# Tokens as the stationary operand in 26 projection calls, an overflow branch ahead of the final norm, and a longer ring for the expert weights

## The chip, the cores and the metric

The kernel runs on one core of a Trainium2 chip. The metric is the device time of one execution, in microseconds (us). Before the change it is 1512.69 us, the median of 3 runs (1511.3 to 1512.91). The engines are called PE (TensorE matmul; PEld is its weight load), DVE (VectorE), ACT (ScalarE), POOL (GpSimd) and SP (SyncE, which here issues almost all DMAs).

## The reference, cut to what matters

The program computes two decoder layers over 256 tokens of width 1024, all in float32, and a last RMSNorm. Layer 0 ends in a dense SwiGLU, layer 1 in a top-2-of-8 expert SwiGLU.

```python
for layer in range(DEPTH):                       # DEPTH = 2
    h = rms_norm(x, norm_mix[layer])
    # nine projections of h: q, f, i, g (1024 wide), b, c, u (1024), gate_a, gate_b (1024)
    ...
    o = rms_norm(hgrn2(q, k, i, log_f), g_norm_w) * silu(g)
    y_a = o @ w_proj_hgrn
    y_b = (c * causal_conv3(b * u)) @ w_proj_conv
    merged = sigmoid(gate_a) * y_a + sigmoid(gate_b) * y_b
    x = x + merged @ w_out
    h = rms_norm(x, norm_ffn[layer])
    if layer % 2 == 0:
        x = x + (silu(h @ dense_w1) * (h @ dense_w3)) @ dense_w2        # D_FF = 2816
    else:                                        # each token goes to 2 of 8 experts
        x = x + sum_e gates[:, e] * ((silu(h @ w1[e]) * (h @ w3[e])) @ w2[e])
return rms_norm(x, final_norm)
```

The weights are 414 MB in float32, 277 MB of them the experts'.

## The kernel before

**Dense products.** A weight matrix is read in pieces of 1 MB. `wload` (line 77) takes a buffer from a ring (`from_ring`), issues the DMA on SP's queue, and splits the piece into a high part on ACT (line 91, tile `whi`) and a low part on DVE (line 93, tile `wlo`). The activations are split the same way (`hh`, `hl`), so each product is three matmuls: high by high, high by low, low by high. There are two forms.

- `mm_cols` (line 125): 128 x 128 of the weights are stationary and the 256 tokens move through them. The result has the output columns on the partitions (tile `psb`). One call on 512 columns is 8 k-tiles x 4 column blocks x 3 parts = 96 matmuls, each 256 wide.
- `mm_toks` (line 151): 128 x 128 of the activations are stationary and 512 weight columns move. The result has the tokens on the partitions (tile `psa`): 8 k-tiles x 2 token halves x 3 parts = 48 matmuls, each 512 wide.

Before, `mm_toks` serves the HGRN value and output-gate projections and `w_out`. `mm_cols` serves the rest: forget gates, queries, the convolution's b, c, u, the two merge gates (lines 577 to 583), the two projections (lines 620 to 637) and the dense w1 and w3 (lines 713 to 723). The down projection of the dense layer (`down`, line 700) has its own loops of 512-wide matmuls.

In the column form the factor `rstd` of a token lies along the free axis, so DVE multiplies by a broadcast row (`by_rbc`, line 256) ahead of the sigmoid or silu. In the token form it is one number per partition and rides in the ACT instruction as its scale.

**Buffers.** Matmul results come from a PSUM tag `mm` with two buffers. The split weights come from `his` (three buffers, tag `hi`) and `los` (two, tag `lo`). A scheduler lays the instructions of each engine out in a fixed order; each engine, and SP's queue, takes them in that order.

**The expert layer.** `moe` (line 775) sorts the experts into eight slots `q` with room for 96 or 64 tokens each (96, 64, 96, 96, 64, 96, 96, 64). Tokens are gathered by one-hot matmuls (`gather`, for slot 0, and at slots 0, 3 and 6 for the next up to three slots), the weights stream as moving operands straight from their raw pieces (`up_proj` line 975, `down` line 987), and the results are scattered back by one-hot matmuls (`scatter` line 1007). A slot reads 34.6 MB whatever its room. The pieces lie in a ring of raw buffers; a piece's DMA is issued on SP as soon as PE has finished with the buffer's last piece. From line 781 on the ring has 11 buffers: the four of `raws`, and the tags qq, fc, v, tokA, sg8, kk and tokB of the large tiles that are free by then. The tag kk holds `xw` of the router (line 458) until then.

**The end.** After the last scatter `finish` (line 754) makes the last norm and writes the output in four DMAs on SP. Then every engine loads two counts (line 1067): they say whether any expert had more tokens than its slot has room for. If so, `slots(1)` and `slots(2)` are run, each followed by another `finish`. With these inputs neither is. The instructions of the two bodies lie between the branch and its target on every engine.

Of the kernel before, what the change touches and what calls it, by code (L numbers as in the profile page):

```python
# [13 lines left out]
ALU = mybir.AluOpType  # L14
# [22 lines left out]
def trunk_kernel(ctx: ExitStack, tc: tile.TileContext, x, w_in, lower_bounds, hgrn_norm_w, conv_w,  # L37
# [32 lines left out]
    def from_ring(kind, pool, shape, dt):  # L70
        tag = ring[kind][0]
        ring[kind].rotate(-1)
        if tag is None:
            return pool.tile(shape, dt, tag=kind, name="w" + kind)
        return big.tile(shape, dt, tag=tag, name="w" + kind)
# [143 lines left out]
    def transposed(src, j):  # L219
        ps = psum.tile([128, 2, S], F32, tag="so"[j % 2], name="pst")  # L220
# [229 lines left out]
    def route_start(l):  # L450
# [5 lines left out]
        moe_ps["wb"] = big8("bu", [128, D])  # L456
        nc.gpsimd.dma_start(moe_ps["wb"], bc_row(norm_ffn[l], D))
        moe_ps["xw"] = big8("kk", [128, TT, D])
# [20 lines left out]
    def route_rows(t, half):  # L479

        xw, hh, hl = (moe_ps[n] for n in ("xw", "hh", "hl"))
        cs = slice(half * 512, half * 512 + 512)
        nc.vector.tensor_tensor(xw[:, t, cs], xt[:, t, cs], moe_ps["wb"][:, cs], op=ALU.mult)
        nc.scalar.activation(hh[:, t, cs], xw[:, t, cs], AF.Copy)

    def route_low(t, half):
        xw, hh, hl = (moe_ps[n] for n in ("xw", "hh", "hl"))
        cs = slice(half * 512, half * 512 + 512)
        nc.vector.tensor_tensor(hl[:, t, cs], xw[:, t, cs], hh[:, t, cs].bitcast(F32), op=ALU.subtract)
# [25 lines left out]
    def mixer(l):  # L515
# [104 lines left out]
        for g in range(2):  # L620
            ps = mm_cols(w_proj_conv[l], g * 512, 512, ych, ycl)
            gs = slice(g * 4, g * 4 + 4)
            nc.vector.tensor_tensor(sg[8][:, gs, :], sg[8][:, gs, :], ps, op=ALU.mult)
# [6 lines left out]
        mh, ml = (big8(tag, [128, KT, S], F32R) for tag in ("hlC", "hlD"))  # L630
        for g in range(2):
            ps = mm_cols(w_proj_hgrn[l], g * 512, 512, oh, ol)
            for i in range(2):
                gs = slice(g * 4 + i * 2, g * 4 + i * 2 + 2)
                nc.vector.tensor_tensor(sg[7][:, gs, :], sg[7][:, gs, :], ps[:, i * 2:i * 2 + 2, :], op=ALU.mult)
                nc.vector.tensor_tensor(sg[7][:, gs, :], sg[7][:, gs, :], sg[8][:, gs, :], op=ALU.add)
                split(sg[7][:, gs, :], mh[:, gs, :], ml[:, gs, :])
# [3 lines left out]
        for g in range(2):  # L641
# [10 lines left out]
            if g == 0:  # L652
                ps = mm_toks(w_out[l], 0, mh, ml)
# [35 lines left out]
    def dense(l):  # L689
# [22 lines left out]
        lo_, hi_ = slice(0, 512), slice(512, 1024)  # L712
        for ci, (c0, n) in enumerate(FCH):
            nt = n // 128
            pa = mm_cols(dense_w1[j], c0, n, hh, hl, enter if ci == 0 else {})
            sa = big8(("fc", "kk")[ci % 2], [128, nt, S])
            by_rbc(sa, pa)
            nc.scalar.activation(sa, sa, AF.Silu)
            pb = mm_cols(dense_w3[j], c0, n, hh, hl)
            nc.vector.tensor_tensor(sa, sa, pb, op=ALU.mult)  # L720
            ah = big8(("qq", "v")[ci % 2], [128, nt, S], F32R)
            al = big8(("bu", "sg7")[ci % 2], [128, nt, S], F32R)
            split(sa, ah, al)
# [5 lines left out]
            else:  # L729

                def add(dh):
                    cs = (lo_, hi_)[dh]
                    for t in range(TT):
                        nc.vector.scalar_tensor_tensor(xt[:, t, cs], ys[t * 2 + dh], rstd[:, t:t + 1], xt[:, t, cs],
                                                       op0=ALU.mult, op1=ALU.add)
# [15 lines left out]
            pend = (c0, n, ah, al)  # L751


    def finish():
# [4 lines left out]
        for t in range(TT):  # L759
            for dh in range(2):  # L760
# [3 lines left out]
                nc.sync.dma_start(osrc[:, t, cs], fin[:, t, cs])  # L764
# [10 lines left out]
    def moe(l):  # L775
# [5 lines left out]
        less("kk")  # L781
        more("kk", "tokB")
# [4 lines left out]
        cnt = consts.tile([128, 1], F32, name="cnt")  # L787
# [28 lines left out]
        def late():  # L816
# [31 lines left out]
            for i in range(2):  # L848
# [4 lines left out]
                nc.vector.tensor_reduce(cnt, over, axis=AX.X, op=ALU.max)  # L853
                nc.vector.tensor_copy(orderi[:, i:i + 1], cnt)
# [32 lines left out]
        ids = {0: 0}  # L887

# [6 lines left out]
        def slots(base):  # L895
# [91 lines left out]
            def down(q, c0, n, th, ys):  # L987
# [12 lines left out]
                if c0 + n == FF:  # L1000
                    y = los.tile([128, 2, 3 * 256], F32R, tag="lo", name="y")
# [5 lines left out]
            def scatter(q, y):  # L1007
                PT = one_hot_t(q)
                for dh in range(2):
                    cs = slice(dh * 512, dh * 512 + 512)  # L1010
                    for t in range(TT):
# [15 lines left out]
                        if q == NE - 1:  # L1027
                            square(t, dh, "kk")
# [8 lines left out]
            for q in range(NE):  # L1037
                xf = xfs[q]
                ys = [psum.tile([128, 512], F32, tag="o", name="ye") for _ in range(2 if CAPS[q] == 96 else 1)]
                for ci, (c0, n) in enumerate(ECH):  # L1040
# [6 lines left out]
                    up_proj(expert_w3, c0, n, pb, xf, q)  # L1047
                    if ci == 1:
# [4 lines left out]
                    sa = his.tile([128, ng, n // 4], F32, tag="hi", name="sae")  # L1053
                    nc.scalar.activation(sa, pa[:, 0:ng, 0:n // 4], AF.Silu)  # L1054
                    nc.vector.tensor_tensor(sa, sa, pb[:, 0:ng, 0:n // 4], op=ALU.mult)  # L1055
                    th = his.tile([128, nb, ng, 32], F32, tag="hi", name="the")
# [52 lines left out]
```

## Time and profile before

| what | us |
|---|---|
| median of 3 runs | 1512.69 |
| the profiled execution's own time | 1511.85 |
| its span, first to last instruction | 1510.1 |
| PE busy in the span | 1462.3 |
| DVE / ACT / POOL busy | 651.4 / 394.4 / 41.7 |
| start of the first expert matmul | 809.4 |
| start of the last expert piece's first matmul | 1489.2 |

The profiled execution takes 1.75 us more than its span; the median of the runs lies 0.84 us above it. The table of slices on the page shows two parts. Up to about 810 us PE is busy throughout and the DMA engines about half. From there on the DMA engines are busy nearly throughout, at some 410 GB/s, and PE as well by its busy time; but a matmul's record reaches to its modelled end, so a busy PE may still be waiting for weights between two matmuls.

### The profile page before, as it was taken

Reading aid. Unit: us, or ns where it says so; the run is one execution under the profiler, and the core shown is the slowest. Engines: PE = TensorE matmul, PEld = TensorE weight load, DVE = VectorE, ACT = ScalarE, POOL = GpSimd, SP = SyncE. Lnnn points to the kernel's source line nnn. Section 1 sums busy time; section 2 is a strip of 40 time slices with the busy share of each in tenths; the row PEclk is TensorE's granted clock in tenths of the full one; section 3 lists DMA queues with packets and bytes.
Section 4 is the critical chain, followed back from the end, with each engine's and each line's share of the span. In section 5 each row is a group of like instructions: output and inputs, shape, how many; then the busy total and the mean of one; then the engine's idle time right before and its main releaser. Section 6 shows DMA issues by size and latency. Waiting matters only on the chain.

```text
span 1510.1 us, 39658 instructions
## 1 busy us (share of the span) xinstructions
PE 1462.3 (97%) x18130; PEld 1203.4 (80%) x18130; DVE 651.4 (43%) x875; ACT 394.4 (26%) x484; POOL 41.7 (3%) x80
## 2 busy tenths in 40 slices
PE   7999999999999999999999999899999989999994
PEld 7989999999999998999996696557977554766751
DVE  6965776665455796568764202011121102011112
ACT  6544334454344554434442000000000000000000
POOL 3000011000000000001000000000000000000000
PEclk9999999999999999999999999999999999999998
DMA  8564544556556555555746899999999999999994
GB/s 270 181 194 157 169 140 170 194 168 195 186 178 197 166 194 170 168 168 203 285 168 226 290 402 409 410 413 406 411 373 402 408 413 409 408 412 359 411 410 184
DMA packets 135364, 418.15 MB, mean 277 GB/s; under 512 B 6784, under 2 KB 8928, under 8 KB 123920
## 3 DMA queue, kind: packets, MB, share of 16 engines
q1 hardware_dynamic: 134768, 414.26, 73.9%
q8 instruction: 146, 2.39, 0.7%
q0 software_dynamic: 384, 1.21, 0.3%
q14 instruction: 34, 0.28, 0.1%
q10 hardware_dynamic: 32, 0.01, 0.0%
HBM read 414.40 MB, written 1.05 MB: 275 GB/s over the span
## 4 chain that ended last, share of the span: by engine, by line
PE 89%; DMA 9%; DVE 1%; ACT 0%; issue 0%; SPq 0%; POOL 0%; POOLq 0%; DVEq 0%; ACTq 0%
PE psb L139 12%; PE pa L982 12%; PE psb L143 12%; PE psb L141 12%; PE pb L982 11%; PE ye L972 10%; DMA wraw<-in_expert_w_dram 8%; PE psa L160 3%; PE psa L162 3%; PE psa L161 3%; PE psc L1023 2%; PE y L708 1%; PE y L709 1%; PE y L710 1%; PE pg L920 1%; PE ye L964 1%
## 5 line engine op out<-in xcount | busy, mean ns | idle before, releaser
L139 PE MATMUL psb<-hlA,whi 128*128 128x256 f32 x1376 | 393.5, 286 | 3.2 <-ACT whi L91 3.2
L143 PE MATMUL psb<-hlA,wlo 128*128 128x256 f32 x1376 | 390.4, 284 | 0.8 <-DVE wlo L93 0.8
L141 PE MATMUL psb<-hlB,whi 128*128 128x256 f32 x1376 | 390.2, 284 | 0.0
L91 ACT ACTIVATE whi<-wraw 128x2048 fp32r<-128x2048 f32 (+1 forms) x165 | 251.7, 1543 | 376.6 <-PE psb L141 234.5
L93 DVE TENSOR_TENSOR wlo<-wraw,whi 128x2048 fp32r<-128x2048 f32 (+1 forms) x165 | 297.9, 1821 | 116.3 <-issue 40.4
L139 PEld LDWEIGHTS psb<-hlA,whi 128*128 128x128 f32 x1376 | 264.3, 192 | 4.6 <-ACT whi L91 3.6
L143 PEld LDWEIGHTS psb<-hlA,wlo 128*128 128x128 f32 x1376 | 264.2, 192 | 1.5 <-DVE wlo L93 1.3
L141 PEld LDWEIGHTS psb<-hlB,whi 128*128 128x128 f32 x1376 | 264.5, 192 | 0.5
L1055 DVE TENSOR_TENSOR sae<-sae,pb 128x768 f32<-128x768 f32 (+3 forms) x24 | 19.1, 796 | 454.5 <-PE pb L982 454.5
L972 PE MATMUL ye<-wraw,the 128*32 128x256 f32 x2640 | 150.5, 379 | 1.0 <-issue 1.0
L972 PEld LDWEIGHTS ye<-wraw,the 128*32 128x32 f32 x2640 | 104.8, 110 | 39.9 <-issue 2.5
L1054 ACT ACTIVATE sae<-pa 128x768 f32<-128x768 f32 (+3 forms) x24 | 16.4, 685 | 433.1 <-PE pa L982 433.1
L982 PE MATMUL pb<-wraw,bu 128*32 128x256 f32 (+1 forms) x2112 | 109.3, 362 | 2.4 <-DMA wraw<-in_expert_w_dram 1.8
L982 PE MATMUL pa<-wraw,bu 128*32 128x256 f32 (+1 forms) x2112 | 110.0, 362 | 0.7 <-DMA wraw<-in_expert_w_dram 0.7
L982 PE MATMUL pb<-wraw,hlD 128*32 128x256 f32 (+1 forms) x1920 | 100.8, 362 | 4.0 <-DMA wraw<-in_expert_w_dram 3.9
L982 PE MATMUL pa<-wraw,hlD 128*32 128x256 f32 (+1 forms) x1920 | 102.2, 362 | 0.7 <-DMA wraw<-in_expert_w_dram 0.7
L982 PEld LDWEIGHTS pb<-wraw,bu 128*32 128x32 f32 x2112 | 74.7, 110 | 34.3 <-issue 2.8
L982 PEld LDWEIGHTS pa<-wraw,bu 128*32 128x32 f32 x2112 | 73.2, 110 | 34.0 <-issue 4.9
L982 PEld LDWEIGHTS pb<-wraw,hlD 128*32 128x32 f32 x1920 | 71.3, 110 | 30.3 <-DMA wraw<-in_expert_w_dram 5.8
L982 PEld LDWEIGHTS pa<-wraw,hlD 128*32 128x32 f32 x1920 | 72.8, 110 | 26.3 <-issue 6.4
L964 PE MATMUL ye<-wraw,the 128*64 128x512 f32 x264 | 61.8, 601 | 10.7 <-DMA wraw<-in_expert_w_dram 10.7
L964 PEld LDWEIGHTS ye<-wraw,the 128*64 128x64 f32 x264 | 17.2, 136 | 51.2 <-issue 27.1
(259 smaller groups left out, 1459.3 us busy)
## 6 DMA issues: line engine op xcount, KB each, us to landing
wraw<-in_expert_w_dram SPq DMA_DIRECT2D x216, 1024.0 KB, 17.8
wraw<-in_w_in_dram SPq DMA_DIRECT2D x72, 1024.0 KB, 5.2
wraw<-in_expert_w_dram SPq DMA_DIRECT2D x64, 768.0 KB, 15.9
wraw<-in_dense_w_dram SPq DMA_DIRECT2D x33, 1024.0 KB, 5.1
wraw<-in_w_proj_conv_dram SPq DMA_DIRECT2D x8, 1024.0 KB, 5.1
wraw<-in_w_proj_hgrn_dram SPq DMA_DIRECT2D x8, 1024.0 KB, 5.1
wraw<-in_w_out_dram SPq DMA_DIRECT2D x8, 1024.0 KB, 5.2
xt<-in_x_dram SPq DMA_DIRECT2D x2, 512.0 KB, 3.8
```

Source lines behind the costliest of these rows:

```text
L91: nc.scalar.activation(hf[:, ks], rf[:, ks], AF.Copy)
L93: nc.vector.tensor_tensor(lf[:, ks], rf[:, ks], hf[:, ks].bitcast(F32), op=ALU.subtract)
L139: nc.tensor.matmul(o, wh[:, k, cs], hh[:, kt, :], start=first, stop=False, skip_group_check=True)
L141: nc.tensor.matmul(o, wh[:, k, cs], hl[:, kt, :], start=False, stop=False, skip_group_check=True)
L143: nc.tensor.matmul(o, wl[:, k, cs], hh[:, kt, :], start=False, stop=last, skip_group_check=True)
L160: nc.tensor.matmul(o, hh[:, kt, ts], wh[:, k, :], start=kt == 0, stop=False)
L161: nc.tensor.matmul(o, hh[:, kt, ts], wl[:, k, :], start=False, stop=False)
L162: nc.tensor.matmul(o, hl[:, kt, ts], wh[:, k, :], start=False, stop=kt == KT - 1)
L964: nc.tensor.matmul(out[64 * h:64 * h + 64, 0:n], stat, w[:, h * n:h * n + n], start=start, stop=stop, skip_group_check=True)
L972: nc.tensor.matmul(out(g)[32 * lane:32 * lane + 32, 0:n], by_lane(g if lane == 3 else lane, lane), w[:, c0:c0 + n], start=start and g != 1 ...
L982: nc.tensor.matmul(ps[32 * lane:32 * lane + 32, g, 0:n // 4], xf[:, kt, 32 * g:32 * g + 32], w[:, k, lane * n // 4:(lane + 1) * n // 4], s ...
L1023: nc.tensor.matmul(ps[:, o], PT[:, w, ts], y[:, part, c], start=i == part == 0, stop=part == 1 and i in (0, 3), skip_group_check=True)
```

## The change

- The two merge gates, the two projections and the five 512-wide chunks of dense w1 and w3 use `mm_toks` in place of `mm_cols`: 4 + 4 calls in each layer and 10 in the dense layer, 26 in all. Sigmoid and silu take `rstd` as ACT's scale, read PSUM and write SBUF.
- What then has tokens on its partitions but is wanted as a stationary operand with columns on them is transposed by PE: the merged branch (`merged`, 4 groups of 4 transposes in each layer, at k-tiles 3 and 5 of the second `w_proj_hgrn` call and at k-tiles 1 and 2 of the first `w_out` call), and each dense chunk (`turn`, 8 transposes at k-tile 3 of the next chunk's w1 call). The transposed tiles are split out of PSUM.
- The dense layer's `rstd` goes into w3's eviction in place of the last addition.
- The router's `xw` shrinks to half a row and shares a tile with `wb`, so kk stays in the ring. In `moe` sg8 leaves the ring (it takes the scattered results `y`), and the three `hi` buffers come in: 13 buffers where there were 11. The tiles `sa` and `th` move from `his` to two tiles of `los`.
- Overflow is told in one number (0, 1 or 2). One branch on it stands ahead of `finish`, with the second nested in it, and there is one `finish`. Its DMAs go half to SP, half to ACT. The last slot scatters one token half after the other.

```diff
-        less("kk")
-        more("kk", "tokB")
+        less("sg8")
+        more("hi", "hi", "hi", "tokB")
+        work = [los.tile([128, 2, 768], F32, tag="lo", name="work") for _ in range(2)]
...
-            sg[s] = big8(f"sg{s}", [128, KT, S])
+            sg[s] = big8(f"sg{s}", [128, TT, D])
             for g in range(2):
-                ps = mm_cols(wi, col(s, g), 512, hh, hl)
-                gs = slice(g * 4, g * 4 + 4)
-                by_rbc(sg[s][:, gs, :], ps)
-                nc.scalar.activation(sg[s][:, gs, :], sg[s][:, gs, :], AF.Sigmoid)
+                ps = mm_toks(wi, col(s, g), hh, hl)
+                for t in range(TT):
+                    nc.scalar.activation(sg[s][:, t, g * 512:g * 512 + 512], ps[:, t, :], AF.Sigmoid, scale=rstd[:, t:t + 1])
...
+        def merged(j):
+            ps = transposed(sg[7], j, "s")
+            split(ps, mh[:, 2 * j:2 * j + 2, :], ml[:, 2 * j:2 * j + 2, :])
+
         for g in range(2):
-            ps = mm_cols(w_proj_hgrn[l], g * 512, 512, oh, ol)
...
+            ps = mm_toks(w_proj_hgrn[l], g * 512, oh, ol,
+                         {3: [lambda: merged(0)], 5: [lambda: merged(1)]} if g == 1 else {})
+            for t in range(TT):
+                cs = slice(g * 512, g * 512 + 512)
+                nc.vector.tensor_tensor(sg[7][:, t, cs], sg[7][:, t, cs], ps[:, t, :], op=ALU.mult)
+                nc.vector.tensor_tensor(sg[7][:, t, cs], sg[7][:, t, cs], sg[8][:, t, cs], op=ALU.add)
+        late_cols = {1: [lambda: merged(2)], 2: [lambda: merged(3)]}
...
-                ps = mm_toks(w_out[l], 0, mh, ml)
+                ps = mm_toks(w_out[l], 0, mh, ml, late_cols)
...
+        def turn(pend):
+
+            c0, n, sa, ah, al = pend
+            ps = psum.tile([128, 4, S], F32, tag="mm", name="pst")
+            for k in range(4):
+                for t in range(TT):
+                    nc.tensor.transpose(ps[:, k, t * 128:t * 128 + 128], sa[:, t, k * 128:k * 128 + 128], ident)
+            for i in range(2):
+                split(ps[:, 2 * i:2 * i + 2, :], ah[:, 2 * i:2 * i + 2, :], al[:, 2 * i:2 * i + 2, :])
...
+            if n == 512:
+                pa = mm_toks(dense_w1[j], c0, hh, hl, steps)
+                for t in range(TT):
+                    nc.scalar.activation(sa[:, t, :], pa[:, t, :], AF.Silu, scale=rstd[:, t:t + 1])
+                pb = mm_toks(dense_w3[j], c0, hh, hl)
+                for t in range(TT):
+                    nc.vector.scalar_tensor_tensor(sa[:, t, :], pb[:, t, :], rstd[:, t:t + 1], sa[:, t, :],
+                                                   op0=ALU.mult, op1=ALU.mult)
...
-                nc.sync.dma_start(osrc[:, t, cs], fin[:, t, cs])
+                (nc.sync, nc.scalar)[dh].dma_start(osrc[:, t, cs], fin[:, t, cs])
...
+                    if q == 4 and ci == 1 and base == 0:
+                        left.append(nc.values_load(orderi[0:1, 0:1], min_val=0, max_val=2))
...
         slots(0)
+        with tc.If(left[0] > 0):
+            slots(1)
+            with tc.If(left[0] > 1):
+                slots(2)
         finish()
-        left = [nc.values_load(orderi[0:1, i:i + 1], min_val=0, max_val=S) for i in range(2)]
-        for base in (1, 2):
-            with tc.If(left[base - 1] > 0):
-                slots(base)
-                finish()
```

How the order of instructions moves is shown at three places. The first is PE in the dense layer, chunk 1's w1 call (hlA, hlB are the split activations). Before, around its middle:

```order
L139 MATMUL psb<-hlA,whi 128x256
L141 MATMUL psb<-hlB,whi 128x256
L143 MATMUL psb<-hlA,wlo 128x256
L139 MATMUL psb<-hlA,whi 128x256
L141 MATMUL psb<-hlB,whi 128x256
```

And now, where `turn` of chunk 0 (its product in fc) stands in it:

```order
L163 MATMUL psa<-wlo,hlA 128x512
L164 MATMUL psa<-whi,hlB 128x512
L727 MATMUL pst<-ident,fc 128x128 x8
L162 MATMUL psa<-whi,hlA 128x512
L163 MATMUL psa<-wlo,hlA 128x512
```

Each matmul is twice as wide, there are half as many, and eight transposes stand between the two weight pieces of the call.

The second is DVE in layer 0 around `w_proj_hgrn` (sg_1156 is sg[7], the merged branch; hlD its low part). Before:

```order
L623 TENSOR_TENSOR sg_1426<-sg_1426,psb 128x1024
L93 TENSOR_TENSOR wlo<-wraw,whi 128x2048 x2
L635 TENSOR_TENSOR sg_1156<-sg_1156,psb 128x512 x2
L636 TENSOR_TENSOR sg_1156<-sg_1156,sg_1426 128x512 x2
L93 TENSOR_TENSOR wlo<-wraw,whi 128x2048
L56 TENSOR_TENSOR hlD<-sg_1156,hlC 128x512 x2
```

Now:

```order
L625 TENSOR_TENSOR sg_1330<-sg_1330,psa 128x2x512
L95 TENSOR_TENSOR wlo<-wraw,whi 128x2048 x2
L643 TENSOR_TENSOR sg_1156<-sg_1156,psa 128x512 x2
L644 TENSOR_TENSOR sg_1156<-sg_1156,sg_1330 128x512 x2
L95 TENSOR_TENSOR wlo<-wraw,whi 128x2048
L56 TENSOR_TENSOR hlD<-pst,hlC 128x512 x2
L95 TENSOR_TENSOR wlo<-wraw,whi 128x2048
L643 TENSOR_TENSOR sg_1156<-sg_1156,psa 128x512 x2
L644 TENSOR_TENSOR sg_1156<-sg_1156,sg_1330 128x512 x2
L56 TENSOR_TENSOR hlD<-pst,hlC 128x512 x2
```

The operations and their sizes are the same, but the low part is now taken from PE's transposed tile `pst`, and before the second pair (L643, L644) a weight split stands.

The third is DVE at the end of the program. Before, from the last scatter's split to the first branch:

```order
L56 TENSOR_TENSOR y<-ye,y 128x512
L1025 SCALAR_TENSOR_TENSOR xt<-psc,qgates,xt 128x512 x4
L196 SCALAR_TENSOR_TENSOR rstd<-msq 128x1
L762 SCALAR_TENSOR_TENSOR bu<-xt,rstd,wbf 128x512
L196 SCALAR_TENSOR_TENSOR rstd<-msq 128x1
L762 SCALAR_TENSOR_TENSOR bu<-xt,rstd,wbf 128x512 x3
L1067 TENSOR_LOAD orderi
L1069 COMPARE_AND_BRANCH
```

Now, from the same split on; the branch jumps over both bodies to what the next block shows:

```order
L1099 STREAM_TRANSPOSE work<-work 128x6x32 x2
L56 TENSOR_TENSOR sg_13795<-ye,sg_13795 128x512
L1062 SCALAR_TENSOR_TENSOR xt<-psc,qgates,xt 128x512 x4
L1086 TENSOR_LOAD orderi
L1107 COMPARE_AND_BRANCH
```

```order
L1109 UNCONDITIONAL_BRANCH x2
L1107 UNCONDITIONAL_BRANCH
L198 SCALAR_TENSOR_TENSOR rstd<-msq 128x1 x2
L791 SCALAR_TENSOR_TENSOR bu<-xt,rstd,wbf 128x512 x4
L1144 UNCONDITIONAL_BRANCH
```

The load of the count and the branch stand between the last addition and the norm, on every engine, though the source asks for the load in slot 4.

## Rows read from the trace of the kernel before

**Rows 1.** The page: busy times, and DMA rate in 40 slices of 37.75 us.

```profile
PE 1462.3 (97%) x18130; PEld 1203.4 (80%) x18130; DVE 651.4 (43%) x875; ACT 394.4 (26%) x484; POOL 41.7 (3%) x80
GB/s 270 181 194 157 169 140 170 194 168 195 186 178 197 166 194 170 168 168 203 285 168 226 290 402 409 410 413 406 411 373 402 408 413 409 408 412 359 411 410 184
```

**Rows 2.** Longest wait of PE from 10 to 809 us: total, times, longest.

```profile
PE psb L139 <- ACT whi L91: 3.2, 1, 3.2
```

**Rows 3.** Timeline of PE (start, us, instruction): 42 wide steps, then 53 narrow ones.

```profile
359.78 0.39 PE L710 MATMUL y<-whi,bu 128*128 128x512 f32 x1
...
369.30 0.39 PE L710 MATMUL y<-whi,bu 128*128 128x512 f32 x1
369.53 0.28 PE L139 MATMUL psb<-hlA,whi 128*128 128x256 f32 x1
...
375.88 0.28 PE L143 MATMUL psb<-hlA,wlo 128*128 128x256 f32 x1
```

**Rows 4.** Timeline of PE: eight transposes within a token call.

```profile
304.93 1.04 PE L224 MATMUL pst<-ident,xt 128*128 128x128 f32 x8
305.72 0.48 PE L160 MATMUL psa<-whi,hlC 128*128 128x512 f32 x1
306.04 0.40 PE L161 MATMUL psa<-wlo,hlC 128*128 128x512 f32 x1
```

**Rows 5.** Timeline of DVE after a `w_proj_hgrn` call (start, us, instruction).

```profile
288.77 1.28 DVE L635 TENSOR_TENSOR sg<-sg,psb 128x512 f32<-128x512 f32 x2 [3.42 <-PE psb L143]
289.98 1.29 DVE L636 TENSOR_TENSOR sg<-sg,sg 128x512 f32<-128x512 f32 x2
291.18 2.29 DVE L93 TENSOR_TENSOR wlo<-wraw,whi 128x2048 fp32r<-128x2048 f32 x1
```

**Rows 6.** A group by line and form: busy us, mean ns, idle before.

```profile
L562 ACT ACTIVATE v<-psa,rstd 128x512 f32<-128x512 f32 x8 | 5.1, 686 | 13.7 <-PE psa L162 13.7
```

**Rows 7.** Stretches of 30 us in the expert layer: busy, PEclk, DMA share, GB/s.

```profile
850.00:880.00 30.00, 30.00 (x555) 24.46 (x551) 6.57 (x10) 1.58 (x4) 0.00 (x0) 1.00 0.76 276
1030.00:1060.00 30.00, 29.89 (x649) 26.39 (x645) 2.13 (x4) 0.65 (x1) 0.00 (x0) 1.00 1.02 409
1110.00:1140.00 30.00, 29.96 (x560) 24.52 (x562) 6.42 (x10) 1.58 (x4) 0.00 (x0) 1.00 0.92 353
1370.00:1400.00 30.00, 30.00 (x578) 22.45 (x580) 4.37 (x10) 1.37 (x4) 0.00 (x0) 1.00 0.92 349
```

**Rows 8.** Timeline of SP's queue: expert pieces 11 and 12 to 14 are issued.

```profile
806.01 0.37 SPq L99 DMA_DIRECT2D wraw<-in_expert_w_dram  x1
812.26 5.55 SPq L99 DMA_DIRECT2D wraw<-in_expert_w_dram  x3
```

**Rows 9.** Timeline of the end, from the last scatter's matmuls on.

```profile
1491.88 2.14 PE L1023 MATMUL psc<-y,st 128*128 128x512 f32 x8 [0.76 <-ACT y L55]
1493.36 2.73 DVE L1025 SCALAR_TENSOR_TENSOR xt<-psc,qgates,xt 128x512 f32<-128x512 f32 x4 [0.81 <-PE psc L1023]
...
1496.41 0.16 DVE L196 SCALAR_TENSOR_TENSOR rstd<-msq 128x1 f32<-128x1 f32 x1 [0.32 <-ACT junk L191]
...
1497.30 0.75 DVE L762 SCALAR_TENSOR_TENSOR bu<-xt,rstd,wbf 128x512 f32<-128x512 f32 x1 [0.73 <-POOL rstd L197]
1499.23 1.41 DVE L762 SCALAR_TENSOR_TENSOR bu<-xt,rstd,wbf 128x512 f32<-128x512 f32 x2 [0.45 <-POOL rstd L197]
```

**Rows 10.** The instructions of lines 1069, 1104, 764: ns min/median/max, first and last start.

```profile
L1069 DVEq COMPARE_BRANCH  x2: 56/64/72, 1499.9 to 1503.5; - x2
L1069 DVEq EVENT_SEMAPHORE  x2: 21/21/21, 1503.0 to 1506.6; - x2
L1069 SPq EVENT_SEMAPHORE  x16: 17/17/17, 1504.8 to 1508.5; - x16
L1104 SPq EVENT_SEMAPHORE  x13: 17/28/28, 1508.6 to 1510.1; - x13
DMA to landing us min/median/max: 2.9/3.9/4.2
```

More of the change, by code (lines that the diff above doesn't have):

```diff
@@ L74, in from_ring @@
             return pool.tile(shape, dt, tag=kind, name="w" + kind)
+        if tag == "hi":
+            return his.tile(shape, dt, tag=tag, name="w" + kind)
         return big.tile(shape, dt, tag=tag, name="w" + kind)
@@ L217, in to_cols, with transposed @@
         return hh, hl
-    def transposed(src, j):
-        ps = psum.tile([128, 2, S], F32, tag="so"[j % 2], name="pst")
+    def transposed(src, j, tag=None):
+        ps = psum.tile([128, 2, S], F32, tag=tag or "so"[j % 2], name="pst")
         for i in range(2):
@@ L712, in dense @@
         lo_, hi_ = slice(0, 512), slice(512, 1024)
+        def turn(pend):
[6 more added lines that the diff above has]
+                split(ps[:, 2 * i:2 * i + 2, :], ah[:, 2 * i:2 * i + 2, :], al[:, 2 * i:2 * i + 2, :])
         for ci, (c0, n) in enumerate(FCH):
             nt = n // 128
[L715 to L720, printed above, removed]
+            steps = dict(enter) if ci == 0 else {3: [lambda p=pend: turn(p)]}
+            pend = pend and (*pend[:2], *pend[3:])
+            sa = big8(("fc", "kk")[ci % 2], [128, TT, n])
             ah = big8(("qq", "v")[ci % 2], [128, nt, S], F32R)
             al = big8(("bu", "sg7")[ci % 2], [128, nt, S], F32R)
-            split(sa, ah, al)
+            if n == 512:
[6 more added lines that the diff above has]
+                                                   op0=ALU.mult, op1=ALU.mult)
+            else:
+                sa = sa.rearrange("p t c -> p (t c)").rearrange("p (k s) -> p k s", s=S)
+                pa = mm_cols(dense_w1[j], c0, n, hh, hl, steps)
+                by_rbc(sa, pa)
+                nc.scalar.activation(sa, sa, AF.Silu)
+                pb = mm_cols(dense_w3[j], c0, n, hh, hl)
+                by_rbc(sa, sa)
+                nc.vector.tensor_tensor(sa, sa, pb, op=ALU.mult)
+                split(sa, ah, al)
             if ci == 0:
@@ L758, in finish @@
             make_rstd(slice(t, t + 1))
-        for t in range(TT):
             for dh in range(2):
@@ L786, in moe @@
         gates = consts.tile([128, TT, NE], F32, name="gates")
-        cnt = consts.tile([128, 1], F32, name="cnt")
+        more_ = consts.tile([128, 2], F32, name="more")
         tmp = consts.tile([128, TT, NE], F32, name="rtmp")
@@ L887, in moe @@
         ids = {0: 0}
+        left = []
         def weights(src, q):
@@ L1000, in down @@
                 if c0 + n == FF:
-                    y = los.tile([128, 2, 3 * 256], F32R, tag="lo", name="y")
+                    y = big8("sg8", [128, 2, 3 * 256], F32R)
                     split(ys[0], y[:, 0, 0:512], y[:, 1, 0:512])
@@ L1008, in scatter @@
                 PT = one_hot_t(q)
-                for dh in range(2):
-                    cs = slice(dh * 512, dh * 512 + 512)
-                    for t in range(TT):
+                steps = [(dh, t) for dh in range(2) for t in range(TT)]
+                if q == NE - 1:
+                    steps.sort(key=lambda s: s[1])
+                if True:
+                    for dh, t in steps:
+                        cs = slice(dh * 512, dh * 512 + 512)
                         ts = slice(t * 128, t * 128 + 128)
@@ L1052, in slots @@
                     ng, nb = CAPS[q] // 32, n // 128
-                    sa = his.tile([128, ng, n // 4], F32, tag="hi", name="sae")
+                    half = work[turns[0] % 2]
+                    turns[0] += 1
+                    sa = half[:, 0, 0:ng * n // 4].rearrange("p (g c) -> p g c", g=ng)
                     nc.scalar.activation(sa, pa[:, 0:ng, 0:n // 4], AF.Silu)
                     nc.vector.tensor_tensor(sa, sa, pb[:, 0:ng, 0:n // 4], op=ALU.mult)
-                    th = his.tile([128, nb, ng, 32], F32, tag="hi", name="the")
+                    th = half[:, 1, 0:nb * ng * 32].rearrange("p (b g s) -> p b g s", b=nb, g=ng)
                     for g in range(ng):
```

35 lines of the change are left out of this document (16 added, 19 removed).

## Prediction

> **What bounds the kernel now.** I read the page first, then the list of waits, then the rates. The page shows PE busy for 97% and the DMA rate in two parts: up to slice 21 (about 800 us) under 300 GB/s, then about 410 [rows 1]. In the first part PE is the bound: from 10 to 809 us its longest wait is a single one of 3.2 us [rows 2], and everything else in the list is shorter. What PE saves there moves the start of the expert layer, and what PE is made to wait there is lost.
>
> In the second part neither engine is the bound alone. DMA runs at 409 GB/s in a steady stretch, but there are three dips: 276, 353 and 349 GB/s over 30 us each [rows 7]. They lie where PE turns the one-hots and gathers tokens (slots 0, 3 and 6): it takes up no weights, the ring is full, SP can issue nothing. DMA stood still for 30 x (409 - 276) / 409 = 9.8 us, then 30 x 56 / 409 = 4.1 us and 30 x 60 / 409 = 4.4 us. After each dip the slots with room for 64 tokens eat pieces faster than they come, and PE waits. So the path is: PE to the first dip; then DMA, the next two dips (8.5 us) added; then the tail behind the last piece.
>
> **The change part by part.**
>
> *Token form.* 26 calls of 96 narrow matmuls become 48 wide ones, so 26 x 48 = 1248 pairs of narrow ones become 1248 wide. Between the first and last wide row lie 42 steps in 9.52 us, 0.2267 us each; between the narrow rows 53 in 6.35 us, 0.1198 each, 0.2396 the pair [rows 3]. The pair saves 0.0129 us, in all 16.1 us.
>
> [...]
>
> *Transposes.* Added are 32 for the merged branch (4 x 4 in each of two layers) and 40 for the dense chunks (5 x 8). Eight within a token call hold PE from 304.93 to 305.72, and the matmul behind them takes 0.32 us to the next start instead of 0.23 [rows 4]: 0.88 us for eight, 0.11 each. 72 x 0.11 = 7.9 us, all on PE's path.
>
> *New waits of PE.* In `w_proj_hgrn` the transposes wait for DVE, and all of PE's matmuls are queued behind them. DVE's four operations on a result took 288.77 to 291.18, 2.4 us, and a weight split 2.3 us [rows 5]. The order has a weight split ahead of them, so they end some 4.9 us after the call's end. The transposes of the first half come after 24 wide matmuls, 5.4 us: no wait. In layer 0 those of the second half come after 19 (4.3 us): a wait of 0.6 us. I take 1 us for both layers with what the two splits behind them add; the bounds are 0 and, if DVE is one split (2.3 us) late each time, 4.6 us. In the dense layer `turn` comes 5.4 us after w3's end and needs two operations and one split, 3.6 us: covered. `turn` takes the third tile of a tag with two buffers, but the order has w3's first matmul wait for DVE, not ACT, so it takes `turn`'s buffer and not that of w1's result, whose silu would just have begun.
>
> *Evictions.* Sigmoid and silu now read PSUM themselves, two per call at 0.686 us, as the value projection's do [rows 6]. Those calls show no wait of PE, so this is priced at nothing; its cover is the 5.4 us of the next half call. The broadcast multiply that DVE loses was not on the path. The smaller `xw`, the moved `rstd`, `y` in sg8 and `sa`, `th` in `los` move no operation on the path: nothing.
>
> Sum of the first part: 16.1 - 7.9 - 1.0 = 7.2 us earlier at the first expert matmul.
>
> *Ring.* 13 buffers for 11. A piece of 1.05 MB at 409 GB/s is 2.56 us. Before, the eleventh piece was issued at 806.01, into kk, and the twelfth at 812.26, into the buffer that PE's first piece had left [rows 8]. Now kk is free earlier and the `hi` buffers come free with the last matmuls of `w_out`, so the ring is full when PE starts and stays so to the first dip. Then DMA is 2 pieces further on: 5.1 us. At the second and third dip it has the same 5.1 us more room, and these were 4.1 and 4.4 us long, so they close: 8.5 us more. Together 13.6 us. The bounds: 0, if the two buffers are not what the dips hang on, and all three dips, 18.3 us. I take 13.6: with the dips closed, DMA runs through to the last piece.
>
> *The end.* The norm comes behind the branch. DVE's first branch was at 1499.9 and its next instruction at 1503.0; the second pair is 1503.5 and 1506.6: a jump costs 3.1 us [rows 10]. The first branch was taken while the last two multiplies (1499.23 to 1500.64 [rows 9]) still ran, so the sequencer does not wait for its engine. So I let DVE load the count when its last addition is handed over, which is when PE's last scatter matmul ends, 1494.0 on the clock of before [rows 9], add 0.5 us for the load and 3.1 for the jump, and get 1497.6 for both `rstd`; 0.9 us to the first multiply (1496.41 to 1497.30, a pow of POOL between), 4 x 0.75 for four, 1501.5. A DMA landed 3.9 us after its issue [rows 10]: 1505.5. Then 1.5 us, what SP's last instructions took (1508.6 to 1510.1). That is 1507.0 where it was 1510.1: the two jumps of SP behind the output, 1504.8 and 1508.5, set the end before. Gain 3.1 us; if DVE's jump only starts after the last addition (1496.09), 1509.1, gain 1.0. I take 2.5, near the row that shows the sequencer ahead. SP's own jump lies ahead of the output now, and ACT's runs beside DVE's.
>
> [...]
>
> **Sum.** 7.2 + 13.6 + 2.5 = 23.3 us. Against the profiled execution's 1511.85: 1488.6. The runs' median lies 0.84 higher: 1489.4, say 1489.5.
>
> **The rivals.**
>
> *A. The wide matmul saves nothing in its new places.* A pair would cost 0.2396 as before, and the transposes and waits stay: the first part is 8.9 us later instead of 7.2 earlier, 1489.5 + 16.1 = 1505.6. Against it: the rows are from `down`, the same shape with the same splits beside it. [...]
>
> *B. The two buffers do not count*, because PE and DMA find another lockstep: 1489.5 + 13.6 = 1503. Against it: the dips are where the ring is full.
>
> *C. More closes*: all three dips, 4.7 us more: 1485.
>
> *D. Slower.* In the token form ACT has to empty PSUM, and ACT's queue is in order. If its two evictions stand behind a weight split that waits for PE, each call's successor but one waits for both, 2 x 0.686 = 1.37 us in 26 calls, 35.7 us: 1489.5 + 35.7 = 1525. It turns the sign from 23.3 / 26 = 0.9 us a call. Against it: eight calls of this kind stand in the kernel before and PE's waits show none.
>
> *E. It does not come through*: A and B together, 1519, or with half of each, about 1512.
>
> **How the numbers follow.** The forecast, 1484.5 to 1495, gets 0.60 by the bounds of waits and tail; A 0.11, B 0.10, C 0.08, D 0.05, E 0.06. A measurement can tell some 0.2%, 3 us, from no change. Faster: 0.60 + 0.11 + 0.10 + 0.08 and a little of E, 0.90; same 0.04; slower 0.06. The range takes in most of C below, B and the nearer half of A above: 1483 to 1505 holds 0.60 + 0.06 + 0.09 + 0.05 = 0.8.
>
> **What would show it.** The first expert matmul near 802 instead of 809.4; the wide step at 0.227 in gates and chunks; PE's waits on DVE before transposes about 1 us in all; the second and third 30 us dips gone and DMA at 409 from the first on; the last piece's matmuls near 1468; DVE's jump at 3 us, and 11 to 13 us from the last addition's end to the end of the span, now 14.0. I would be wrong if dense chunks show PE waiting for ACT, if the dips stay, or if the jumps take longer over the longer body.

## The result

The changed kernel takes 1495.75 us, the median of 4 runs (1494.91 to 1496.42); the kernel before, timed beside it, 1512.19 (1511.3 to 1512.91, 4 runs). The ratio is 0.9879, with a 95% interval of 0.9863 to 0.9896. So it is 1.2% faster, as forecast, with an interval clear of 1. The time lies inside the stated range of 1483 to 1505, but 0.75 us above the narrower 1484.5 to 1495 that was given 0.60: the gain is 16.4 us where the sum had 23.3.

All the runs below, timed again beside the kernel before (1513.3 to 1513.5 there), fit in one table. The program is cut at three marks that every trace has: the first matmul of the value projection (the program's first call in token form), the first expert matmul, and the first matmul on the last expert piece. All in us; the last column is the median of the timed runs, the others are of the profiled execution.

| kernel | start to value projection | to first expert matmul | to last piece | to the end | span | median |
|---|---|---|---|---|---|---|
| before | 61.5 | 747.9 | 679.8 | 20.9 | 1510.1 | 1512.2 |
| changed | 64.7 | 739.8 | 672.0 | 18.2 | 1494.6 | 1495.75 |
| e1 changed, again | 64.2 | 739.7 | 672.5 | 17.8 | 1494.1 | 1495.1 |
| e2 hi once in the ring | 61.6 | 739.7 | 676.1 | 18.1 | 1495.5 | 1499.1 |
| e3 column form | 63.0 | 749.2 | 671.6 | 17.8 | 1501.5 | 1501.4 |
| e4 old end | 65.0 | 739.7 | 672.4 | 21.3 | 1498.4 | 1499.0 |
| e5 14 buffers | 61.8 | 739.7 | 670.8 | 16.7 | 1488.9 | 1490.4 |
| e6 no later gathers | 62.2 | 739.7 | 672.1 | 17.7 | 1491.7 | 1493.4 |
| e7 warm start | 62.2 | 739.6 | 672.5 | 17.9 | 1492.2 | 1494.15 |
| e8 small slot first | 64.4 | 739.2 | 669.7 | 17.8 | 1491.1 | 1492.0 |
| e9 11 buffers | 63.9 | 739.7 | 679.8 | 18.2 | 1501.5 | 1503.0 |
| e10 14, warm | 62.0 | 739.7 | 669.7 | 16.6 | 1488.0 | 1489.7 |
| e11 14, warm, small first | 62.3 | 739.2 | 662.5 | 16.2 | 1480.2 | 1482.6 |
| e12 14, warm, spaced | 62.2 | 739.3 | 665.0 | 17.6 | 1484.1 | 1486.0 |

Before against changed: 3.2 us lost at the start, 8.2 won up to the experts, 7.8 in the stream of pieces, 2.7 at the end; together the 15.5 us between the two spans.

### The profile page after: what moved, and what is told of

Read it like the earlier page. It is cut to its first block, busy times and chain, and to the rows that moved or that the text cites. A ratio compares the mean times of both kernels' runs of the same rounds, so it can differ in the third digit from the quotient of the medians.

```text
span 1494.6 us, 37312 instructions
## 1 busy us (share of the span) xinstructions
PE 1454.8 (97%) x16954; PEld 1125.0 (75%) x16954; DVE 639.3 (43%) x873; ACT 397.0 (27%) x502; POOL 41.2 (3%) x80
## 5 line engine op out<-in xcount | busy, mean ns | idle before, releaser
L141 PE MATMUL psb<-hlA,whi 128*128 128x256 f32 x672 | 194.5, 289 | 3.9 <-ACT whi L93 3.9
L145 PE MATMUL psb<-hlA,wlo 128*128 128x256 f32 x672 | 192.0, 286 | 0.5 <-DVE wlo L95 0.5
L143 PE MATMUL psb<-hlB,whi 128*128 128x256 f32 x672 | 191.8, 285 | 0.0
L162 PE MATMUL psa<-whi,hlA 128*128 128x512 f32 x480 | 189.4, 395 | 0.0
L164 PE MATMUL psa<-whi,hlB 128*128 128x512 f32 x480 | 187.2, 390 | 0.0
L163 PE MATMUL psa<-wlo,hlA 128*128 128x512 f32 x480 | 187.0, 389 | 0.0
L1006 PE MATMUL ye<-wraw,work 128*32 128x256 f32 x2640 | 151.1, 379 | 1.0 <-issue 0.8
L141 PEld LDWEIGHTS psb<-hlA,whi 128*128 128x128 f32 x672 | 130.3, 194 | 5.1 <-ACT whi L93 4.3
L145 PEld LDWEIGHTS psb<-hlA,wlo 128*128 128x128 f32 x672 | 130.3, 194 | 1.1 <-DVE wlo L95 1.0
L143 PEld LDWEIGHTS psb<-hlB,whi 128*128 128x128 f32 x672 | 130.5, 194 | 0.2
L1095 ACT ACTIVATE work<-pa 128x768 f32<-128x768 f32 (+3 forms) x24 | 16.4, 684 | 427.3 <-PE pa L1016 427.3
## 6 DMA issues: line engine op xcount, KB each, us to landing
wraw<-in_expert_w_dram SPq DMA_DIRECT2D x216, 1024.0 KB, 17.9
```

Source lines behind the costliest of these rows:

```text
L141: nc.tensor.matmul(o, wh[:, k, cs], hh[:, kt, :], start=first, stop=False, skip_group_check=True)
L143: nc.tensor.matmul(o, wh[:, k, cs], hl[:, kt, :], start=False, stop=False, skip_group_check=True)
L145: nc.tensor.matmul(o, wl[:, k, cs], hh[:, kt, :], start=False, stop=last, skip_group_check=True)
L162: nc.tensor.matmul(o, hh[:, kt, ts], wh[:, k, :], start=kt == 0, stop=False)
L163: nc.tensor.matmul(o, hh[:, kt, ts], wl[:, k, :], start=False, stop=False)
L164: nc.tensor.matmul(o, hl[:, kt, ts], wh[:, k, :], start=False, stop=kt == KT - 1)
```

## The profile after

Of the page of the changed kernel, PE's busy time and the rate in 40 slices, the lines that answer [rows 1]:

```profile
PE 1454.8 (97%) x16954; PEld 1125.0 (75%) x16954; DVE 639.3 (43%) x873; ACT 397.0 (27%) x502; POOL 41.2 (3%) x80
GB/s 260 180 198 168 173 143 169 171 195 186 183 195 171 179 182 193 169 157 208 288 200 245 280 401 409 410 412 407 410 391 410 407 412 411 407 412 373 410 409 201
```

PE has 1176 matmuls fewer (1248 pairs into one each, 72 transposes more). The first dip stands in slices 22 and 23 as before.

All waits of PE from 65 to 804 us in the changed kernel (total, times, longest; in us):

```profile
PE pg L954 <- DVE sg L915: 0.6, 1, 0.6
PE pr L962 <- ACT rstdb L809: 0.2, 1, 0.2
```

Both are the gather's and stood there before. No transpose and no matmul of the new calls waits for DVE or ACT.

PE in a dense w1 call, around the transposes of the chunk before (start, us, instruction), to be held against [rows 4]:

```profile
373.13 0.39 PE L164 MATMUL psa<-whi,hlB 128*128 128x512 f32 x1
373.37 1.03 PE L727 MATMUL pst<-ident,kk 128*128 128x128 f32 x8
374.16 0.48 PE L162 MATMUL psa<-whi,hlA 128*128 128x512 f32 x1
374.47 0.40 PE L163 MATMUL psa<-wlo,hlA 128*128 128x512 f32 x1
374.70 0.39 PE L164 MATMUL psa<-whi,hlB 128*128 128x512 f32 x1
```

The eight take 0.79 us and the matmul behind them 0.31 to the next start, as in the kernel before; the steps around are 0.23. Over the dense chunks the mean of 431 such steps is 0.2269 us, where the prediction had 0.2267.

The end of the changed kernel, from the timeline (the number in brackets is the idle time before, and what ended it):

```profile
1480.52 2.73 DVE L1062 SCALAR_TENSOR_TENSOR xt<-psc,qgates,xt 128x512 f32<-128x512 f32 x4 [0.79 <-PE psc L1060]
...
1484.10 0.19 ACT L193 ACTIVATION_READ_ACCUMULATOR junk<-xt 128x1 f32 x1
1487.55 0.23 DVE L198 SCALAR_TENSOR_TENSOR rstd<-msq 128x1 f32<-128x1 f32 x2 [4.30 <-ACTq L1107]
1487.86 1.07 POOL L199 TENSOR_TENSOR rstd<-rstd,mhalf 128x1 f32<-128x1 f32 x2 [687.35 <-DVE rstd L198]
1488.44 2.74 DVE L791 SCALAR_TENSOR_TENSOR bu<-xt,rstd,wbf 128x512 f32<-128x512 f32 x4 [0.66 <-POOL rstd L199]
1489.22 1.67 SPq L793 DMA_DIRECT2D out_dram<-bu  x2
1489.88 1.66 ACTq L793 DMA_DIRECT2D out_dram<-bu  x2
```

And the branch of line 1107 on DVE and ACT, and the landing of the output (line 793): duration in ns, first and last start in us.

```profile
L1107 DVEq COMPARE_BRANCH  x1: 72/72/72, 1481.8 to 1481.8; - x1
L1107 ACTq COMPARE_BRANCH  x1: 50/50/50, 1484.1 to 1484.1; - x1
...
L1107 DVEq EVENT_SEMAPHORE  x1: 21/21/21, 1484.8 to 1484.8; - x1
L1107 ACTq EVENT_SEMAPHORE  x1: 17/17/17, 1487.5 to 1487.5; - x1
```

```profile
DMA to landing us min/median/max: 2.1/2.1/2.1
```

DVE jumps in 3.0 us, as forecast. But ACT comes to its branch only when its last sum of squares is under way (1484.1), takes 3.4 us to jump, and the norm waits for that: 1487.55, not 1484.8. In the kernel before ACT's two jumps had taken 0.5 and 2.0 us; the prediction had read DVE's and SP's alone.

## The experiments

**e1 and the start.** The changed kernel once more.

> The changed kernel once more, as the measure for the three beside it. In its first profile the value projection's first matmul started at 64.71 us, in that of the kernel before at 61.48. Theory 'chance': those 3.2 us are the execution's (first landing 1.24 us later, PE's step 0.21 us until 22 us), so this profile may show any start from 61 to 65 us. Rival 'change': the start belongs to the changed kernel, so it is again within 0.5 us of 64.7. From there to the first expert matmul 739.8 us either way.

The start was late again (ratio to before 0.9877, 0.9862 to 0.9892), but in the kernels of e2 to e6, e8 and e9, which share its first 60 us, the mark lies anywhere from 61.6 to 65.0. Two things make it up. The first weight piece landed between 11.2 and 12.8 us. And PE's clock: e4 (65.0) beside e7 (62.2), stretches of 4 us, busy times by engine, then PEclk, DMA share, GB/s:

```profile
14.00:18.00 4.00, 3.55 (x15) 3.13 (x15) 3.92 (x10) 4.00 (x11) 0.00 (x0) 0.50 1.07 372
18.00:22.00 4.00, 4.00 (x20) 4.00 (x20) 3.73 (x9) 3.59 (x7) 0.00 (x0) 0.50 0.74 222
```

```profile
14.00:18.00 4.00, 3.19 (x27) 2.98 (x26) 3.92 (x9) 4.00 (x10) 0.00 (x0) 1.00 1.09 368
18.00:22.00 4.00, 4.00 (x35) 4.00 (x35) 3.51 (x8) 3.70 (x8) 0.00 (x0) 1.00 0.88 276
```

At a granted clock of 0.50 PE issues 20 matmuls in 4 us, at 1.00 it issues 35. PE had idled 2.7 to 3.9 us for the first piece, and how many slow matmuls (0.41 us long instead of 0.28) then follow differs between executions: 13 to 15 in e2, e5 and e6, which start the value projection at 61.6 to 62.2, and 32 to 39 in e3, e4, e8 and e9, which start it at 63.0 to 65.0. The kernel before had 13 (granted clock 0.50 from 13.2 to 16.6 us), the changed one 35 (its trace has no record of the clock before 22.4 us, where the run of slow ones ends and 1.00 begins) and, again, 39. So the 3.2 us are chance, and the profile of before had a lucky start.

**e7, a warm start.**

```diff
+        if l == 0:
+            dummy = psum.tile([128, 4, 128], F32, tag="mm", name="dummy")
+            for i in range(44):
+                nc.tensor.transpose(dummy[:, i % 4, :], ident, ident)
```

> The changed kernel with 44 transposes of the identity into an unused tile, on PE between the first transposes of x and the first product; their results are not read. Theory 'the start is a matter of the clock': PE's step stays at 0.12 us from the first product on, the value projection's first matmul starts at 60 to 61.5 us, so up to 3.5 us faster than an execution with a cold start. Rival 'the start is a matter of the landings': the start stays within 0.7 us of the landing-bound one, no gain that can be measured. Rival 'in the way': the 44 transposes end after the first piece has been split, and the start is later.

PE keeps a granted clock of 1.00, its matmuls 0.28 us, and in all four kernels with such transposes (e7, e10 to e12) the start is 62.0 to 62.3. The 44 hold PE until 14.4 us, some 1.5 us after the product could have begun (the first piece was there at 12.2, and elsewhere the first product follows it by 0.7), so both the first theory (the step) and the last rival (in the way) were partly right. In the medians it can't be told from nothing: 1494.15 against 1495.1.

**e3, the column form back** in gates, projections and dense chunks (their lines as before the change).

> The changed kernel with gates, projections and dense chunks back in the column form; ring and end as changed. Theory 'wide saves': from the value projection's first matmul to the first expert matmul 747.9 us instead of 739.8, so 8.2 us slower in all. Rival 'the start belongs to the token form': the start is back at 61.5 us and the whole is only 4.9 us slower. Rival 'the expert layer hides it' (DMA is the bound there): the first expert matmul 8.2 us later but the end less than 4 us later.

Up to the experts 749.2, 9.5 us more. Of these 1.3 are PE's clock, which in this execution fell just ahead of the first expert matmul (the same columns):

```profile
805.60:808.90 3.30, 3.30 (x17) 3.30 (x16) 2.00 (x10) 0.69 (x2) 0.70 (x1) 0.50 0.51 207
```

8.2 remain, as between before and changed. They go through: the stretch of the experts is as long as with the token form (671.6), since DMA, its ring full, waits at its beginning for PE's first matmuls (in the changed kernel the thirteenth piece landed 2.6 us before them, the fourteenth was issued 2.9 us behind). The start (63.0) is one of those that the token form shows too, so it doesn't belong to the form. In the medians e3 is 5.7 to 6.3 us slower than the two of the changed kernel, less than 8.2; they take in the starts, which differ by more than what is missing.

**e9, 11 buffers, all free in time.**

```diff
-        less("sg8")
-        more("hi", "hi", "hi", "tokB")
+        less("sg8", "kk")
+        more("hi", "hi", "hi")
```

> The changed kernel with 11 buffers that are all free before PE's first expert matmul (tokB and kk left out, the three hi buffers in); every buffer is taken again after 11 pieces, throughout. With 11 buffers of which two came late, the kernel before took 679.8 us from the first expert matmul to the last piece's; 13 took 672.0 to 672.5. Theory 'two pieces at the first dip and nothing behind': 677.5, 5.1 us more than 13, and the other 2.3 us of the ring's gain were the two buffers that came late. The prediction as it was put, the second and third dip come back whole: 672.3 + 13.6 = 685.9. Rival 'only being free in time counts': 672 to 673.5.

679.8: to a tenth of a us what the kernel before took with its two late buffers. So being free in time is worth nothing by the end, the count everything: 7.3 to 7.8 us for two buffers. That is between the first theory and the prediction. Landing of some pieces (counted from 1), in us after the first expert matmul, from the traces:

```
piece                      13     41    121    151    231    261    280
before, 11               11.8   91.4  289.1  363.3  560.2  635.3  679.7
e9, 11 in time           11.7   91.2  288.8  363.8  560.8  636.0  679.7
changed, 13              -2.6   86.7  284.3  357.1  554.2  628.9  671.9
e6, 13, no later gathers -1.9   86.6  284.4  357.3  554.3  628.2  672.1
e5, 14                   -5.7   83.8  281.5  355.7  552.8  626.2  670.8
```

Two buffers put the stream 4.5 us ahead behind the first dip (piece 41), 2 more behind the second (121 to 151), 1 more from the third on. An earlier try, e2, had aimed at the same, with the tag hi once in the ring instead of three times:

> The changed kernel with 11 buffers in the ring instead of 13 (two of the three hi buffers left out). The prediction as it was put: 13.6 us slower (5.1 at the first dip, 8.5 because the second and third come back). Reading of the trace by pieces: 7.8 us slower (4.7 at the first dip, 1.5 at the second, 1.5 at the third). Rival 'the buffers don't count': within 1 us.

3.7 to 4.2 us longer in the stretch. It doesn't answer the question: hi still rotates over three buffers, and the loads into the other two were laid out far ahead, so 13 pieces stood ready at the start (the thirteenth landed 2.2 us before the first expert matmul) and only later was the ring shorter.

**e6, the later gathers left out.**

```diff
-                        if q in (0, 3, 6):
-                            xfs += gather(q + 1, min(3, NE - 1 - q), "bu" if q == 3 else "hlD")
+                        if q == 0:
+                            xfs += gather(q + 1, 3, "hlD")
+                            xfs += [xfs[1], xfs[2], xfs[3], xfs[1]]
```

> Leaves out part of the computation: the gathers in slots 3 and 6 are not made, slots 4 to 7 take the tokens of slots 1 to 3 once more. The ring has 13 buffers. Theory 'the later dips are PE's gather stops': the second and third dip are gone and the last piece comes some 3 us earlier against the first expert matmul than with the gathers, no more, since DMA is the bound then. Rival 'the later dips come from somewhere else': dips of about 2 us stay at the same pieces.

Half of the theory holds, the dips are gone; the other half doesn't, for nothing is won. The rival, dips at the same pieces, falls. The second and third stretch that answer [rows 7], for e9, the changed kernel and e6, in this order:

```profile
1104.00:1134.00 30.00, 30.00 (x558) 24.50 (x554) 6.50 (x10) 1.58 (x4) 0.00 (x0) 1.00 0.91 343
1364.00:1394.00 30.00, 29.77 (x553) 21.53 (x545) 4.91 (x10) 1.42 (x4) 0.00 (x0) 1.00 0.93 353
```

```profile
1105.00:1135.00 30.00, 29.77 (x619) 23.93 (x617) 3.60 (x7) 0.65 (x1) 0.00 (x0) 1.00 1.00 388
1365.00:1395.00 30.00, 29.66 (x628) 21.58 (x630) 2.58 (x6) 0.65 (x1) 0.00 (x0) 1.00 0.97 375
```

```profile
1102.00:1132.00 30.00, 30.00 (x651) 22.45 (x647) 2.21 (x5) 0.65 (x1) 0.00 (x0) 1.00 1.02 409
1362.00:1392.00 30.00, 29.19 (x638) 21.74 (x630) 2.13 (x4) 0.65 (x1) 0.00 (x0) 1.00 1.02 410
```

With 13 buffers, bytes for 1.5 and 2.5 us are still missing beside 409 GB/s, and without the gathers none. Yet the pieces land when they land anyway: the two rows of the table are never more than 0.7 us apart, and 0.1 at the end. What e6 moves more there it moves less elsewhere: 388 GB/s from 1422 to 1442 us, where the changed kernel has 410 in the same stretch behind its mark. So a dip in the mean rate is not a delay of the same size. With 11 buffers 4.8 and 4.1 us of bytes were missing, and the delay that the two more buffers took away was about 2 and 1.

The times of issue and landing say more. In a steady stretch 6 to 8 pieces are issued and not yet landed. At the first dip that number falls to 0 (46 to 48 us behind the first expert matmul, before, changed and e9 alike), and DMA does stand still. At the second and third it never falls below 2 before, 1 in e9, 3 in the changed kernel and 6 in e6: there was always a piece under way, so DMA did not stand still, it ran slower.

No row here tells the 16 DMA engines apart, so why a dip costs less than its bytes was not shown.

**e4, the end of before** (the norm and four DMAs on SP, then two branches, each with a norm of its own behind it).

> The changed kernel with the end of the kernel before: the norm and its four DMAs on SP ahead of two branches, each with a norm of its own behind it. Theory 'SP's jumps behind the output set the end': 20.9 us instead of 18.2 from the last piece's first matmul to the end of the span, 2.7 us slower. Rival 'the gain at the end is the scatter's order and ACT's queue, not the branch': both stay or go by themselves, 1 us or less; the last slot's order by token halves stays in this kernel.

21.3 us instead of 18.2, and 3 to 4 in the medians. Line 1112 is the second branch, 1147 the program's end, then the output's landing:

```profile
L1112 SPq EVENT_SEMAPHORE  x8: 17/17/17, 1496.3 to 1496.7; - x8
...
L1147 SPq EVENT_SEMAPHORE  x13: 17/28/28, 1496.8 to 1498.3; - x13
...
DMA to landing us min/median/max: 3.3/4.2/5.1
```

SP comes out of its second jump at 1496.3, and 2 us later all is over: SP sets the end, as the prediction read it from [rows 10]. The order of the last scatter stays in this kernel and gives nothing (20.9 before). ACT's queue went with the branch here; what it is worth by itself was not tried.

**e5, 14 buffers.** The scattered results go to three small tiles that are free by then.

```diff
-        less("sg8")
...
-                    y = big8("sg8", [128, 2, 3 * 256], F32R)
+                    y = [big.tile([128, 512], F32R, tag=tag, name="y") for tag in ("st00", "st11")]
...
+                        y.append(big.tile([128, 2, 256], F32R, tag="st12", name="y2"))
```

> The changed kernel with 14 buffers: the scattered results lie in three small tiles, so sg8 stays in the ring. Theory 'room': the first dip shortens by one piece, 2.56 us, the second and third by what is left of them, up to 1.5 us each: 2.5 to 5 us faster. Rival 'the rest of the later dips is not room': 2.56 us faster and the second and third dip as with 13. Rival 'saturated': within 1 us.

2.9 us ahead behind the first dip, 1.2 of it left at the end (2.2 to 2.8 in e10), and the tail behind the last piece 1.1 to 1.5 shorter. The tail is no matter of the ring's room: ACT's jump took 1.8 us here where it took 3.4 and 3.0 in the two profiles of the changed kernel (1.4 to 1.8 in all four kernels with 14 buffers, 2.7 to 3.4 in all with the new end and fewer); why was not tried. The ratio to before is 0.9849, interval 0.9833 to 0.9866, some 5 us below the changed kernel; part of that, in the profiled execution 2.4 us or more, is the start. e10 adds the warm start, with 34 transposes:

> 14 buffers, and 34 transposes (not 44) ahead of the first product to hold PE's clock. If the two effects add: value projection's first matmul at 60.5 to 61.5 us, 739.7 us from there to the first expert matmul, 670.8 to the last piece, 17 to the end: span 1488 to 1489, median about 1490. Rival 'the warm start brings nothing on top': start at 62 to 64, as without.

The sum came (span 1488.0), though the start was later than in the theory (62.0) and the stream 1.1 us shorter. The start lies in the rival's range, and in the medians e10 is no different from e5 (1489.7 and 1490.4), so the rival is not ruled out.

**e8, e11, e12, the order of the slots.** What is left of the first dip hangs on slot 0: with room for 96 PE takes 2.59 us a piece, DMA 2.5. These kernels pin expert 2, that is, give it slot 0 whatever the counts; it has 53 tokens with these inputs. The program pins expert 0. With inputs that give expert 2 more than 64, the overflow branch would run.

```diff
-RANKS = (0, 1, 4, 5, 2, 6, 7, 3)
+RANKS = (0, 3, 4, 1, 5, 6, 7, 2)
...
-                        if q in (0, 3, 6):
-                            xfs += gather(q + 1, min(3, NE - 1 - q), "bu" if q == 3 else "hlD")
+                        if q % 2 == 0:
+                            xfs += gather(q + 1, min(2, NE - 1 - q), "bu" if q % 4 else "hlD")
```

> The changed kernel with another order of the slots: expert 2 (53 tokens with these inputs) is the pinned one and slot 0 has room for 64, so the rooms are 64, 96, 96, 64, 96, 96, 96, 64; tokens are gathered for two slots at slots 0, 2, 4 and 6. Theory 'the first dip is there because slot 0 eats slower than DMA brings': it goes, PE drains the ring in slot 0, and the end comes about 5 us earlier (then PE's own work in the three slots of 96 is the bound). Rival 'it only moves': the dip appears in slots 4 to 6 with the same length, within 1 us of the changed kernel. Rival 'slower': the fourth gather, 5.6 us of PE, lies where PE is the bound.

> 14 buffers, the warm start, and the slots in the order of rooms 64, 96, 96, 64, 96, 96, 96, 64 with expert 2 pinned. With 13 buffers this order took 669.7 us from the first expert matmul to the last piece and had one piece come 6.4 us late in slot 6, where the ring was full behind three slots of 96. Theory 'room': that gap shortens by 2.5 us or more: 666 to 667.5, median about 1486. Rival 'PE is the bound there': 669 to 670 as before, median about 1489.

> 14 buffers, the warm start, expert 2 pinned, and rooms 64, 96, 96, 64, 96, 96, 64, 96: no three of 96 in a row, but the last slot is of 96. Theory 'the ring never fills, so DMA runs through': 660 to 664 us from the first expert matmul to the last piece, and the tail is 3 to 4 us longer (20 matmuls of the last scatter instead of 8): median 1483 to 1487. Rival 'the tail eats it': the last slot's own work is late against the last landing, 1489 or more.

In e8 piece 41 lands 13 us earlier than in the changed kernel (73.4), but in slot 6, behind three slots of 96, the ring is full, one piece comes 6.4 us late, and 2.3 to 2.8 us are left at the end: between the theory's 5 and the rival that it only moves. The fourteenth buffer is worth 7.2 us there (e11 against e8), more than its theory had; and with 14 buffers the order is worth 7.2 (e11 against e10). The stretch is 662.5, and the median of 1482.6 us, ratio 0.9798 (0.9782 to 0.9814), beats both kernels. In the changed kernel the list of PE's waits from 800 to 1480 us has 5.7, 1.4 and 0.7 us for pieces and 3.1 more that it puts down to SP. All that it has for e11, from 801 to 1466:

```profile
PE pb L1019 <- issue: 1.8, 3, 0.8
PE psc L1064 <- ACT y L55: 0.8, 1, 0.8
PE ye L1009 <- issue: 0.6, 1, 0.6
PE ye L1001 <- DMA wraw<-in_expert_w_dram: 0.6, 1, 0.6
```

In e12 the last piece had landed 5.9 us before PE came to it (1460.6 and 1466.5): PE's own work in the last slot of 96 is the bound, the mechanism of the rival, though at 1486.0 it is milder than put there and the median lies in the theory's range.

## Why the prediction was right, and where its sum was wrong

- **Token form: right.** 16.1 less 7.9 is 8.2, and 8.2 was measured. The wait of 1.0 us for DVE did not come: no wait is listed. Evictions and `turn` were covered, as said. Rivals A and D fall with e3 and the list of waits.
- **First expert matmul near 802: 804.5.** The step that failed is the clock zero: I measured from the start of the span, and the first 60 us differ by up to 3.5 us between executions. A mark behind the start would have given 739.8 against a forecast of 740.7. The last piece's matmuls, near 1468 in the forecast, start at 1476.4: 3.2 us later by the start and 5.8 by the ring, 1.0 earlier by the token form.
- **Ring, first dip: right.** 5.1 was forecast; 4.5 to 4.7 came. The later buffers' early issue, which I counted as part of the reason, adds nothing (e9).
- **Ring, second and third dip: the mis-sized term.** 8.5 us forecast, about 3 measured. The step that failed reads "DMA stood still for ... 4.1 us and ... 4.4 us" and then counts that time as delay. DMA did not stand still there: at least 2 pieces were always under way in the kernel before. By the rates, the prediction's own sign, the dips shrank to 388 and 375 GB/s and did not close; by the landings nothing was left to close (e6 gains nothing more), but they had never been worth their missing bytes.
- **The whole distance.** With the first dip, the ring's sum of 13.6 fell short by 5.8 us. Token form and end brought 1.0 and 0.2 more than forecast, the start of the profiled execution lost 3.2: together 7.8, from 23.3 to the 15.5 between the spans. The forecast put the median 0.84 us above the profiled execution, and it lies 0.55 below. So the 6.3 us between 1489.5 and 1495.75 are one mis-sized term; the rest, chance for the most part, nearly cancels.
- **End: right in sum, 2.7 for 2.5, wrong in one step.** 11.4 us from the last addition's end to the end of the span lies in the 11 to 13 forecast. But I let the norm start on DVE's jump and had ACT's run beside it at no cost. ACT's starts 2.3 us later, takes 3.4 us and holds the norm; output DMAs that land in 2.1 us instead of 3.9, two on each queue instead of four on SP's, gave that back, so the sum is right by luck.
- Rival B, no gain from the buffers, falls with e9; C, more than forecast, with the landings; E with both. E's "half of each" is mis-added besides: 1489.5 and half of 29.7 is 1504.4, not 1512.

## What to carry to other kernels

Here a dip in the mean DMA rate bounded what a longer queue could win from above, and no more (4.8 and 4.1 us of bytes missing at the later dips, about 2 and 1 won); what it costs is read from the landings behind it, one row of the trace against another, and from how many transfers are under way in it. Where a stream is held by its consumer, first ask which stretch of the consumer is slower than the stream and whether a fast stretch can stand ahead of it: here two buffers won 7.3 to 7.8 us, and one more together with another order of the slots 9.5. Measure stages between marks inside the program, not from the start of the span.

## What the hardware showed that I had not expected

- After 2.7 to 3.9 us of waiting 13 to 39 of PE's matmuls took 0.41 us each in place of 0.28 (granted clock 0.50 in the kernel before and in e4), and how many differed between executions of one program; work that nobody reads, in the gap, kept the clock at 1.00 and the matmuls at 0.28 (e7).
- Jumps over the untaken bodies took 3.0 us on DVE, 3.4 on ACT and 3.7 on PE in the changed kernel, each by itself. DVE's stayed at 2.8 to 3.1 in every kernel with this end, ACT's lay between 1.4 and 3.4.
- In the stream of e5 ten pieces, 21 to 29 apart, each landed 3.5 to 4.1 us behind the one ahead instead of 2.5. That is some 15 us of the 671, and other runs show the like, smaller and more often (e1 has fifteen of 3.0 to 3.3 behind piece 50). What it is was not tried.
